# Layer 0's modulation tiles in a pool of their own, and the first pair's exponentials beside the v projection

## Chip, cores and metric

The kernel runs on one core of a Trainium2 chip. The metric is the device time of one execution in microseconds. Before the change it is 2110.99 us, the median of three runs from 2109.61 to 2111.64.

## What is computed

A block of four layers over 256 latent tokens and 256 context tokens of width 1024, with mixers A, B, C, A, each followed by a squared-ReLU MLP; every sub-layer has an RMSNorm, and shift, scale and gate come from a modulation product `silu(c) @ ada_w[l] + ada_b[l]`. The change is in mixer A, a bidirectional chunkwise mLSTM with 8 heads, chunks of 128 tokens and a scan in each direction. Cut to what matters:

```python
def mlstm_chunk_scan(q, k, v, log_i, log_f, state, with_output):
    def step(carry, inp):
        C, n, m = carry
        qc, kc, vc, li, lf = inp
        b = jnp.cumsum(lf, axis=-1)
        ...
        C_new = decay[..., None, None] * C + jnp.einsum('bhs,bhsk,bhsv->bhkv', ws, kc, vc)
        log_d = jnp.where(tri, b[..., :, None] - b[..., None, :] + li[..., None, :], -jnp.inf)
        d_mat = jnp.exp(log_d - m_comb[..., None])
        sc = jnp.einsum('bhtk,bhsk->bhts', qc, kc) * d_mat
        num = jnp.einsum('bhts,bhsv->bhtv', sc, vc) + a_inter[..., None] * jnp.einsum('bhtk,bhkv->bhtv', qc, C)
        ...

def mlstm_mixer(xc, xl, w_in, w_gate, b_gate, head_g, w_out, ctx_out):
    ...
    return (jax.nn.sigmoid(o) * h.astype(o.dtype)) @ w_out
```

## The kernel before

Every product with weights is done three times over a split in two parts: a weight tile of 128 x 1024 is loaded by SyncE (`w_dma`), cast to its high part by ScalarE (`w_hi`, line 241) and subtracted to its low part by VectorE (`w_lo`, line 246), and three matmuls (`mm3`, lines 390 to 392; for v lines 422 to 424) add high by high, high by low and low by high in one PSUM bank. `w_get(ahead)` makes the splits some tiles ahead; a split by `w_lo` also issues the load of the tile four further on. Weights are numbered in the order of use; in layer 0 the v projection uses 9 to 16 and the eight output-gate chunks use 17 to 24.

There is no scheduler: each engine carries out its instructions in the order in which the program writes them, and waits on semaphores for those of other engines. Tiles live in pools that are opened and closed like a stack on the left or the right side of the memory; a new tile waits for the last users of the tiles that lay in its place.

`mixer_a` of layer 0 projects keys, queries and gates, and then v in two halves of 512 columns (`nh`), each with four weight tiles (`kk`). The four PSUM banks of a half are copied into `vx` by ScalarE (line 789). The banks are taken in turn from six (`bank`); the scan then names its banks itself: the output-gate chunks go into bank 4, the key transposes into bank 5, the scores into 6 and 7.

Beside the projections, `pump` works off the modulation of layer 0. `ada_pe` does 16 of its tiles (`first`, in the pool `first`) on TensorE. `ada_pump` does 12 more (`ada`) as two sums each on VectorE (line 353, 24 in all), reading the tile and the broadcast conditions `cbc` and writing into `junk`; these two lie in the pool `first` as well. The tiles come through a ring of two, each loaded by SyncE when the one before it in its place is done.

`gates` computes the gate rows on 40 partitions in the pool `rows`, and writes two of them to DRAM (`dnm`, `dar`). `scan_load` (lines 882 and 883) issues, on GpSimd, four row loads `rb` and two `ab` for a pair of heads, broadcast to 128 partitions; `scan_qa` (lines 891 and 892) multiplies `ab` by the queries. In layer 0 both were called at the start of `scan`, with tiles in the scan's own pool `as0`, which opens when `rows` and `first` have closed. In layer 3 they have a pool `al3` from the start, and the loads of two pairs are issued in the gate steps.

`scan` goes over four pairs of heads. For a pair and a direction, `weights` adds a triangular mask to each of two `rb` tiles (VectorE, line 957) and takes exponentials of their chunks (ScalarE, line 959). `scores` makes the score matmuls (line 967) and transposes the keys (line 972); `keys_weigh` weighs the transposed keys (VectorE, line 982), `weigh` multiplies the exponentials by the scores (line 990), `states` makes the state products (TensorE, line 1000), `outputs` the outputs (lines 1025 and 1034). `fillers` lays the halves of the output-gate chunks between them, and copies each from bank 4 (line 912). Before the change `scan` began like this:

```python
        if not last:
            self.scan_load(lp, 0, dnm, dar, n, last)
            self.scan_qa(lp, 0, qT, n)
        for d in range(2):
            weights(0, d)
        scores(0)
        next(fill)
        keys_weigh(0)
        for d in range(2):
            weigh(0, d)
```

Of the kernel before, what the change touches and what calls it, by code (L numbers as in the profile page):

```python
# [8 lines left out]
F32 = mybir.dt.float32  # L9
F32R = mybir.dt.float32r  # L10
BF16 = mybir.dt.bfloat16
I32 = mybir.dt.int32
AF = mybir.ActivationFunctionType
ALU = mybir.AluOpType
# [4 lines left out]
D = 1024  # L19
# [11 lines left out]
N_FIRST = 4  # L31
PE_ADA = 32
# [40 lines left out]
def mixer_a_units():  # L73
    return [("k", 0), ("k", 1), ("k", 2), ("k", 3), ("q", 0), ("gate", 0), ("q", 1), ("q", 2), ("q", 3)]
# [133 lines left out]
class Body:  # L208
# [70 lines left out]
    def ada_fetch(self, j):  # L279

        if j < PE_ADA:
            t = self.ada_raw[j] = self.first.tile([128, 1024], F32, tag="first", name=f"first{j}", bufs=N_FIRST)
            (self.nc.sync if j < 16 + N_FIRST else self.nc.gpsimd).dma_start(out=t, in_=self.ada_in[j])

    def ada_rows(self, j, t):
# [76 lines left out]

    def conditions(self, pool):

        self.cbc = pool.tile([128, 2, 1024], F32, name="cbc")
        self.nc.gpsimd.dma_start(out=self.cbc, in_=self.line.unsqueeze(0).to_broadcast([128, 2, 1024]))
        self.junk = pool.tile([128, 1024], BF16, name="junk")

    def new_mod(self, l):
        self.mods[l] = self.modp.tile([128, 48, 2], F32, tag="mod", name=f"mod{l}")  # L370
# [336 lines left out]
    def mixer_a(self, l, i, last):  # L707
        nc, tc = self.nc, self.tc
        full = LT if last else ALL
        n = full.stop  # L710
        units = mixer_a_units()
        with ExitStack() as st:
            ap = self.block_pool(st, f"a{l}", "left")
            qT = ap.tile([128, 4, 512], F32, name="qT")
            kT = ap.tile([128, 4, 512], F32, name="kT")

            def ev_qk(u, o, sl):
                kind, m = units[u]
                if kind == "k":
                    nc.scalar.copy(kT[:, m, sl], o)  # L720
                else:
                    nc.scalar.activation(qT[:, m, sl], o, AF.Copy, scale=0.125)

            n_head = yield 3, ev_qk
            n_head = n_head or 3
            dr = st.enter_context(tc.tile_pool(name=f"ad{l}", bufs=1, space=DRAM))
            av = self.block_pool(st, f"av{l}", "left")
            vx = av.tile([128, 4, 8, 129], F32, name="vx")
            tok = av.tile([128, 3, 4, 64], F32, name="tok")
            if l == 0:  # L730
                saved = self.hin
            else:
                saved = dr.tile([128, 8, n], F32, name="saved")
                nc.gpsimd.dma_start(out=saved, in_=self.h[:, :, :n])
            nc.gpsimd.memset(vx[:, :, :, 128:129], 1.0)
            lp = self.block_pool(st, f"al{l}", "left") if last else None
            rows_ctx = tc.tile_pool(name=f"ar{l}", bufs=1, side="left", reuse_waits="tile")
            rows = rows_ctx.__enter__()
            steps = None

            count = [0]

            def pump():
                if l == 0:
                    count[0] += 1
                    if count[0] % 2 == 0:
                        self.ada_pe()
                    if count[0] > 3:
                        self.ada_pump(2 if count[0] % 4 == 0 else 1, 0, ADA_A)

            for u in range(n_head, len(units)):
                if units[u][0] == "gate":
                    w = self.w_get()
                    o = self.bank()
                    self.unit(o, w, self.x_chunk, ALL, range(4))
                    pump()
                    self.unit(o, w, self.x_chunk, ALL, range(4, NK))
                    steps = self.gates(rows, dr, i, o, last)
                    next(steps)
                    pump()  # L760
                else:
                    self.chunk(u, self.x_chunk, full if units[u][0] == "q" else ALL, ev_qk, pump)
                    pump()
                    if steps is not None:
                        rowt = next(steps)
                        if rowt and last:
                            for pr in range(2):
                                self.scan_load(lp, pr, rowt[3], rowt[4], n, last)
                            self.scan_qa(lp, 0, qT, n)

            for nh in range(2):
                outs = [self.bank() for _ in range(4)]
                for kk in range(4):
                    w = self.w_get()
                    self.v_step(w, 2 * kk, outs, 512)
                    pump()
                    self.v_step(w, 2 * kk + 1, outs, 512)
                    if nh == 0 and kk == 3:
                        u_, er, wr, dnm, dar = rowt
                        tp = self.bank()[:, 0:480].rearrange("p (a c r) -> p a c r", a=3, c=4)  # L780
                        for qi, t_ in enumerate((u_, er, wr)):
                            for tcn in range(4):
                                nc.tensor.transpose(tp[:, qi, tcn, :], t_[:, tcn * 128 : tcn * 128 + 128], self.ident[0:40, 0:40])
                        nc.scalar.copy(tok[:, :, :, 0:40], tp)
                    pump()
                for tcn in range(4):
                    dst = vx[:, tcn, nh * 4 : nh * 4 + 4, 0:128]
                    src = outs[tcn].rearrange("p (h v) -> p h v", h=4)
                    nc.scalar.copy(dst, src)
            rows_ctx.__exit__(None, None, None)  # L790
            if l == 0:
                while self.epos <= PE_ADA:
                    self.ada_pe()
                self.ada_pump(96, 0, ADA_A)
                self.first_ctx.__exit__(None, None, None)
            sp = self.block_pool(st, f"as{l}", "left")
            self.scan(l, i, last, sp, lp or sp, dnm, dar, qT, kT, vx, tok, saved, n)
        res = self.residual(l, 16, n)
        for m in range(3, 8 if last else 5):
            self.chunk(m, self.x_chunk, full, res, ahead=2 if last else 4)  # L800
        yield None if last else (self.x_chunk, res, (5, 6, 7))
# [83 lines left out]
    def scan_qa(self, lp, pr, qT, n):  # L885
        nc = self.nc
        for d in range(2):
# [3 lines left out]
            nc.gpsimd.tensor_copy(dc, a.rearrange("p (c t) -> p c t", c=4)[:, :, e])  # L891
            nc.gpsimd.tensor_tensor(out=a[:, :n], in0=a[:, :n], in1=qT[:, pr, :n], op=ALU.mult)

    def scan(self, l, i, last, sp, lp, dnm, dar, qT, kT, vx, tok, saved, n):


        nc = self.nc
        full = slice(0, n)
        outc = [0, 1] if last else [0, 1, 2, 3]
        nch = len(outc)  # L900
        masks = (self.mask_f, self.mask_b)
        bk = self.banks
        sg = self.h
        cur = self.cur
# [44 lines left out]


        def weights(pr, d):

            for hh in range(2):
                e = cur["D", pr, d, hh]
                col = 32 * d + 2 * pr + hh
                e3 = e.rearrange("p (c t) -> p c t", c=nch)
                nc.vector.tensor_tensor(out=e3, in0=e3, in1=masks[d].unsqueeze(1).to_broadcast(e3.shape), op=ALU.add)
                for c in outc:
                    nc.scalar.activation(e3[:, c, :], e3[:, c, :], AF.Exp, bias=tok[:, 0, c, col : col + 1])

        def scores(pr):

# [127 lines left out]
            )  # L1090

        fill = fillers()
        if not last:
            self.scan_load(lp, 0, dnm, dar, n, last)
            self.scan_qa(lp, 0, qT, n)
        for d in range(2):
            weights(0, d)
        scores(0)
        next(fill)
        keys_weigh(0)  # L1100
# [4 lines left out]
        for pr in range(4):  # L1105
# [15 lines left out]
            if more:  # L1121
                weights(pr + 1, 0)
# [7 lines left out]
            if more:  # L1130
                weights(pr + 1, 1)
                low()
# [370 lines left out]
    def start(self, n_head, evac_head):  # L1503

        nc = self.nc
        self.first_ctx = self.tc.tile_pool(name="first", bufs=1, side="right", reuse_waits="tile")
        self.first = self.first_ctx.__enter__()
        with self.tc.tile_pool(name="start", bufs=1, side="right", reuse_waits="tile") as sp:

            nc.vector.memset(self.cs, 0.0)  # L1510
# [7 lines left out]
            first = []  # L1518
# [94 lines left out]
            nc.gpsimd.tensor_copy(sp.tile([128, 2], F32, name="after"), self.mods[0][:, 4, :])  # L1613
            for s in range(2):
                nc.gpsimd.dma_start(out=line[s].rearrange("(k p) -> p k", p=128), in_=sg[:, 8 * s : 8 * s + 8])
            self.conditions(self.first)
            for j in range(N_ADA):
                self.ada_dma(PE_ADA + j)
            self.modulate2(0, 0, 4)
# [132 lines left out]
```

## Time and profile before

| what | value |
|---|---|
| median of three runs | 2110.99 us |
| lowest and highest run | 2109.61 and 2111.64 us |
| the profiled execution | 2114.74 us |
| its span, first to last instruction | 2113.0 us |
| busy: PE, DVE, ACT, POOL | 97%, 69%, 45%, 4% of the span |
| mean granted clock of TensorE | 0.990 |
| share of PE in the chain that ended last | 92% |

PE is TensorE, PEld its weight loads, DVE VectorE, ACT ScalarE, POOL GpSimd, SP SyncE; a q behind a name is the engine's sequencer. Times are in microseconds from the start of the span. A row of the timeline gives start, duration, engine, line, operation, output and inputs with their shapes, the count of merged instructions, and in brackets how long the engine stood idle before it and who ended that. Neighbouring instructions of an engine overlap a little, so the duration of one is somewhat longer than its distance to the next. The granted clock is 1.00 at 2.4 GHz and 0.50 at 1.2 GHz.

### The profile page before, as it was taken

How to read it: one execution, taken by the hardware profiler on the slowest of the kernel's cores; microseconds unless marked ns; L12 is line 12 of the kernel's file. 1: busy time of each engine (PE TensorE's matmuls, PEld its weight loads, DVE VectorE, ACT ScalarE, POOL GpSimd, SP SyncE). 2: the span in 40 equal slices, each digit the busy share in tenths (PEclk: the TensorE clock that was granted, in tenths of full speed). 3: DMA queues.
4: the chain of work that ended last, by engine and by line, in shares of the span. 5: the costliest groups of instructions: out<-in, count | busy, mean ns of one | idle time of the engine just before them, and what ended most of it. 6: DMA issues, size and time to landing. Idle time of an engine off the chain costs nothing.

```text
span 2113.0 us, 30325 instructions
## 1 busy us (share of the span) xinstructions
PE 2053.4 (97%) x11730; PEld 1751.2 (83%) x11730; DVE 1453.5 (69%) x2652; ACT 948.9 (45%) x1814; POOL 87.0 (4%) x138
## 2 busy tenths in 40 slices
PE   6989999999999999999999999999999999989998
PEld 4767798888889878988888988898888899889997
DVE  5667777787777775677777764467777776576554
ACT  3436653324236685624333343262433435556554
POOL 0123100000000000000000000000000000310000
PEclk9999999999999999999999999999999999999999
DMA  9783245565553104266565433236556533635552
GB/s 300 272 264 103 64 135 179 177 193 185 184 170 119 50 2 138 92 189 189 179 194 175 130 112 98 94 108 189 187 180 197 179 122 104 175 103 180 184 185 91
DMA packets 97025, 326.11 MB, mean 154 GB/s; under 512 B 17760, under 2 KB 18928, under 8 KB 96240
## 3 DMA queue, kind: packets, MB, share of 16 engines
q1 hardware_dynamic: 81184, 293.81, 43.5%
q0 software_dynamic: 15152, 29.83, 4.6%
q8 instruction: 92, 1.51, 0.3%
q10 hardware_dynamic: 544, 0.52, 0.1%
q14 instruction: 53, 0.43, 0.1%
HBM read 319.73 MB, written 4.33 MB: 153 GB/s over the span
## 4 chain that ended last, share of the span: by engine, by line
PE 92%; DVE 3%; DMA 2%; ACT 2%; issue 1%; POOL 0%; SPq 0%; DVEq 0%; ACTq 0%
PE bank L390 25%; PE bank L392 25%; PE bank L391 25%; PE bank L591 2%; PE bank L592 2%; PE bank L594 2%; PE bank L422 1%; PE bank L1348 1%; PE bank L423 1%; PE bank L424 1%; PE bank L1360 1%; DMA ab<-dar 1%; PE bank L1288 1%; PE bank L1025 1%; DVE wlo L246 1%; PE bank L1000 1%
## 5 line engine op out<-in xcount | busy, mean ns | idle before, releaser
L390 PE MATMUL bank<-xh,whi 128*128 128x512 f32 (+1 forms) x1600 | 579.4, 362 | 1.7 <-ACT h L912 1.0
L241 ACT CAST whi<-raw 128x1024 fp32r<-128x1024 f32 x374 | 387.1, 1044 | 421.1 <-PE bank L391 382.8
L391 PE MATMUL bank<-xl,whi 128*128 128x512 f32 (+1 forms) x1600 | 574.4, 359 | 0.2
L392 PE MATMUL bank<-xh,wlo 128*128 128x512 f32 (+1 forms) x1600 | 573.9, 359 | 0.0
L246 DVE TENSOR_TENSOR wlo<-raw,whi 128x1024 fp32r<-128x1024 f32 x374 | 455.6, 1225 | 152.5 <-ACT whi L241 151.9
L353 DVE SCALAR_TENSOR_TENSOR junk<-ada,cbc 128x1024 bf16<-128x1024 f32 x320 | 390.7, 1221 | 18.1 <-DMA ada<-in_ada 13.8
L390 PE MATMUL bank<-hh,whi 128*128 128x512 f32 (+1 forms) x1096 | 384.5, 351 | 0.0
L392 PE MATMUL bank<-hh,wlo 128*128 128x512 f32 (+1 forms) x1096 | 383.9, 350 | 0.0
L391 PE MATMUL bank<-hl,whi 128*128 128x512 f32 (+1 forms) x1096 | 383.9, 350 | 0.0
L390 PEld LDWEIGHTS bank<-xh,whi 128*128 128x128 f32 x1600 | 304.9, 191 | 49.9 <-ACT h L912 1.6
L392 PEld LDWEIGHTS bank<-xh,wlo 128*128 128x128 f32 x1600 | 304.9, 191 | 44.3
L391 PEld LDWEIGHTS bank<-xl,whi 128*128 128x128 f32 x1600 | 305.0, 191 | 44.0 <-DVE xl L945 1.0
L391 PEld LDWEIGHTS bank<-hl,whi 128*128 128x128 f32 x1096 | 207.4, 189 | 27.4
L392 PEld LDWEIGHTS bank<-hh,wlo 128*128 128x128 f32 x1096 | 207.4, 189 | 27.2
L390 PEld LDWEIGHTS bank<-hh,whi 128*128 128x128 f32 x1096 | 207.4, 189 | 27.1
L565 DVE SCALAR_TENSOR_TENSOR h<-bank,mod,h 128x256 f32<-128x256 f32 x280 | 125.6, 479 | 133.1 <-PE bank L392 133.1
L676 DVE TENSOR_TENSOR hl<-q,hh 128x512 fp32r<-128x512 f32 (+1 forms) x137 | 81.5, 595 | 170.5 <-ACT q L675 170.2
L673 ACT ACTIVATE r<-bank 128x512 f32<-128x512 f32 (+1 forms) x137 | 70.8, 517 | 269.2 <-PE bank L392 266.2
L459 ACT ACTIVATE sq<-h 128x256 f32<-128x256 f32 (+1 forms) x74 | 36.0, 487 | 139.4 <-DVE h L565 114.2
L591 PE MATMUL bank<-xh,whi 128*128 128x256 f32 x312 | 81.4, 289 | 3.5 <-ACT xh L527 3.5
L592 PE MATMUL bank<-xh,wlo 128*128 128x256 f32 x312 | 80.2, 285 | 0.0
L674 ACT ACTIVATE hh<-r 128x512 fp32r<-128x512 f32 (+1 forms) x137 | 75.9, 554 | 4.6
(274 smaller groups left out, 2129.3 us busy)
## 6 DMA issues: line engine op xcount, KB each, us to landing
raw<-in_wts SPq DMA_DIRECT2D x374, 512.0 KB, 4.2
ada<-in_ada SPq DMA_DIRECT2D x160, 512.0 KB, 3.5
start<-in_ada SPq DMA_DIRECT2D x16, 512.0 KB, 9.1
first<-in_ada POOLq DMA_DIRECT2D x12, 512.0 KB, 6.0
cbc<-line POOLq DMA_DIRECT2D x4, 1024.0 KB, 7.8
rb<-dnm POOLq DMA_DIRECT2D x16, 256.0 KB, 7.1
ab<-dar POOLq DMA_DIRECT2D x16, 256.0 KB, 12.2
h<-in_hin SPq DMA_DIRECT2D x4, 512.0 KB, 6.8
```

Of the source, the lines that this page charges most:

```text
L241: self.nc.scalar.copy(hi, self.raw[j])
L246: self.nc.vector.tensor_tensor(out=lo, in0=self.raw.pop(j), in1=hi.bitcast(F32), op=ALU.subtract)
L353: nc.vector.scalar_tensor_tensor(out=junk, in0=w, scalar=1.0, in1=self.cbc[:, s, :], op0=ALU.mult, op1=ALU.mult, accum_out=self.mods[l][:, ...
L390: mm(out, lhsT=whi, rhs=xhi, start=first, stop=False)
L391: mm(out, lhsT=whi, rhs=xlo, start=False, stop=False)
L392: mm(out, lhsT=wlo, rhs=xhi, start=False, stop=last)
L565: self.nc.vector.scalar_tensor_tensor(out=self.h[:, m, a:b], in0=o[:, a - sl.start : b - sl.start], scalar=mod[:, gate + m, s : s + 1], in ...
L591: mm(o[:, :T], lhsT=w[0][:, c], rhs=hi[:, sl], start=(k == 0), stop=False)
L592: mm(o[:, :T], lhsT=w[1][:, c], rhs=hi[:, sl], start=False, stop=False)
L673: nc.scalar.activation(r[:, :n], o, AF.Relu)
L674: nc.scalar.activation(hh[:, sl], r[:, :n], AF.Square)
L676: nc.vector.tensor_tensor(out=hl[:, sl], in0=q[:, :n], in1=hh[:, sl].bitcast(F32), op=ALU.subtract)
```

## The change

`first` now holds only `cbc` and `junk`; the ring of modulation tiles for TensorE gets a pool `tiles` that is opened above it and closed, with `rows`, after the first weight tile of v's second half. There the pool `al0` is opened on the left side, and `scan_load` and `scan_qa` of the first pair are called. `weights` is taken apart into `scan_mask` and `scan_exp`, and for the first pair these are called within v's second half: direction 0 behind the third weight tile, direction 1 behind the fourth, in layer 0 and in layer 3. `scan` no longer begins with them. In layer 0 the loop that drained `ada_pe` is gone.

```diff
@@ ada_fetch
-            t = self.ada_raw[j] = self.first.tile([128, 1024], F32, tag="first", name=f"first{j}", bufs=N_FIRST)
+            t = self.ada_raw[j] = self.tiles.tile([128, 1024], F32, tag="first", name=f"first{j}", bufs=N_FIRST)
@@ conditions
-        self.cbc = pool.tile([128, 2, 1024], F32, name="cbc")
+        if pool:
+            self.cbc = pool.tile([128, 2, 1024], F32, name="cbc")
+            self.junk = pool.tile([128, 1024], BF16, name="junk")
         self.nc.gpsimd.dma_start(out=self.cbc, in_=self.line.unsqueeze(0).to_broadcast([128, 2, 1024]))
-        self.junk = pool.tile([128, 1024], BF16, name="junk")
@@ mixer_a, in the loop over v
                     pump()
+                    if nh == 1 and kk == 0:
+                        rows_ctx.__exit__(None, None, None)
+                        if l == 0:
+                            self.tiles_ctx.__exit__(None, None, None)
+                            lp = self.block_pool(st, f"al{l}", "left")
+                            self.scan_load(lp, 0, dnm, dar, n, last)
+                            self.scan_qa(lp, 0, qT, n)
+                    if nh == 1 and kk >= 2:
+                        self.scan_mask(0, kk - 2)
+                        self.scan_exp(0, kk - 2, tok, [0, 1] if last else [0, 1, 2, 3])
                 for tcn in range(4):
                     dst = vx[:, tcn, nh * 4 : nh * 4 + 4, 0:128]
                     src = outs[tcn].rearrange("p (h v) -> p h v", h=4)
                     nc.scalar.copy(dst, src)
-            rows_ctx.__exit__(None, None, None)
             if l == 0:
-                while self.epos <= PE_ADA:
-                    self.ada_pe()
                 self.ada_pump(96, 0, ADA_A)
                 self.first_ctx.__exit__(None, None, None)
             sp = self.block_pool(st, f"as{l}", "left")
-            self.scan(l, i, last, sp, lp or sp, dnm, dar, qT, kT, vx, tok, saved, n)
+            self.scan(l, i, last, sp, lp, dnm, dar, qT, kT, vx, tok, saved, n)
@@ new, taken out of weights
+    def scan_mask(self, pr, d):
+
+        for hh in range(2):
+            e3 = self.cur["D", pr, d, hh].rearrange("p (c t) -> p c t", t=128)
+            mask = (self.mask_f, self.mask_b)[d].unsqueeze(1).to_broadcast(e3.shape)
+            self.nc.vector.tensor_tensor(out=e3, in0=e3, in1=mask, op=ALU.add)
+
+    def scan_exp(self, pr, d, tok, outc):
+
+        for hh in range(2):
+            e3 = self.cur["D", pr, d, hh].rearrange("p (c t) -> p c t", t=128)
+            col = 32 * d + 2 * pr + hh
+            for c in outc:
+                self.nc.scalar.activation(e3[:, c, :], e3[:, c, :], AF.Exp, bias=tok[:, 0, c, col : col + 1])
@@ scan
-        if not last:
-            self.scan_load(lp, 0, dnm, dar, n, last)
-            self.scan_qa(lp, 0, qT, n)
-        for d in range(2):
-            weights(0, d)
         scores(0)
@@ start
+        self.cbc = self.first.tile([128, 2, 1024], F32, name="cbc")
+        self.junk = self.first.tile([128, 1024], BF16, name="junk")
+        self.tiles_ctx = self.tc.tile_pool(name="tiles", bufs=1, side="right", reuse_waits="tile")
+        self.tiles = self.tiles_ctx.__enter__()
...
-            self.conditions(self.first)
+            self.conditions(None)
```

The orders of TensorE, GpSimd and SyncE are the same before and after; those of ScalarE and VectorE change at the end of v, in layers 0 and 3. A number behind an underscore tells buffers apart and is not the same in both programs; the number right behind `whi`, `wlo` or `raw` is that of the weight.

ScalarE in layer 0, from the cast for the second output-gate chunk on, before (`rb` are the exponentials of the first pair, `vx` the copies of v's second half):

```order
L241 CAST whi18_1004<-raw18_824 128x1024
L241 CAST whi19_1041<-raw19_869 128x1024
L241 CAST whi20_1076<-raw20_907 128x1024
L789 COPY vx_528<-bank_84 128x4x128 x4
L959 ACTIVATE rb_1116<-rb_1116,tok_529 128x128 x4
L959 ACTIVATE rb_1118<-rb_1118,tok_529 128x128 x4
L959 ACTIVATE rb_1122<-rb_1122,tok_529 128x128 x4
L959 ACTIVATE rb_1124<-rb_1124,tok_529 128x128 x4
L241 CAST whi21_1185<-raw21_966 128x1024
```

The same place with the change:

```order
L241 CAST whi18_1030<-raw18_827 128x1024
L241 CAST whi19_1067<-raw19_872 128x1024
L915 ACTIVATE rb_1013<-rb_1013,tok_532 128x128 x4
L915 ACTIVATE rb_1015<-rb_1015,tok_532 128x128 x4
L241 CAST whi20_1112<-raw20_910 128x1024
L915 ACTIVATE rb_1019<-rb_1019,tok_532 128x128 x4
L915 ACTIVATE rb_1021<-rb_1021,tok_532 128x128 x4
L800 COPY vx_531<-bank_84 128x4x128 x4
L241 CAST whi21_1192<-raw21_969 128x1024
```

Eight exponentials moved ahead of the cast of weight 20, and all sixteen ahead of the copies of v.

VectorE at the same place, from the last two modulation sums (`junk`) on, before (`kw` are the key weights):

```order
L353 SCALAR_TENSOR_TENSOR junk_372,mod0_146<-ada43_1023,cbc_370 128x1024 x2
L378 TENSOR_TENSOR mod0_146<-mod0_146,vecs_85 128x8
L246 TENSOR_TENSOR wlo20_1077<-raw20_907,whi20_1076 128x1024
L957 TENSOR_TENSOR rb_1116<-rb_1116,cons_86 128x512
L957 TENSOR_TENSOR rb_1118<-rb_1118,cons_86 128x512
L957 TENSOR_TENSOR rb_1122<-rb_1122,cons_86 128x512
L957 TENSOR_TENSOR rb_1124<-rb_1124,cons_86 128x512
L982 TENSOR_TENSOR kw_1177<-bank_84,tok_529 128x512
```

The same place with the change:

```order
L353 SCALAR_TENSOR_TENSOR junk_115,mod0_151<-ada43_1049,cbc_114 128x1024 x2
L379 TENSOR_TENSOR mod0_151<-mod0_151,vecs_85 128x8
L907 TENSOR_TENSOR rb_1013<-rb_1013,cons_86 128x512
L907 TENSOR_TENSOR rb_1015<-rb_1015,cons_86 128x512
L246 TENSOR_TENSOR wlo20_1113<-raw20_910,whi20_1112 128x1024
L907 TENSOR_TENSOR rb_1019<-rb_1019,cons_86 128x512
L907 TENSOR_TENSOR rb_1021<-rb_1021,cons_86 128x512
L998 TENSOR_TENSOR kw_1184<-bank_84,tok_532 128x512
```

The split of weight 20 moved behind the first two of the four masks; nothing else moved.

## Rows read from the trace of the kernel before

**Rows 1.** The page, part 1: busy us of each engine, share, instructions.
```profile
PE 2053.4 (97%) x11730; PEld 1751.2 (83%) x11730; DVE 1453.5 (69%) x2652; ACT 948.9 (45%) x1814; POOL 87.0 (4%) x138
```
**Rows 2.** Timeline of PE, layer 0, start of the scan.
```profile
143.37 0.66 PE L972 MATMUL bank<-cons,kT 128*128 128x128 f32 x4
...
149.10 0.39 PE L392 MATMUL bank<-xh,wlo 128*128 128x512 f32 x1
154.84 0.70 PE L1000 MATMUL bank<-vx,kw 128*64 128x129 f32 x4 [5.35 <-DVE rb L990]
155.77 2.42 PE L1000 MATMUL bank<-vx,kw 128*64 128x129 f32 x20 [0.22 <-DVE rb L990]
...
170.51 0.50 PE L390 MATMUL bank<-xh,whi 128*128 128x512 f32 x1 [1.02 <-ACT h L912]
...
179.26 1.54 PE L1000 MATMUL bank<-vx,kw 128*64 128x129 f32 x24
```
**Rows 3.** Waits of DVE, 125 to 150: total us, times, longest.
```profile
DVE junk L353 <- DMA ada<-in_ada: 9.8, 3, 3.7
```
**Rows 4.** Timeline of DVE, layer 0, start of the scan.
```profile
148.31 1.22 DVE L246 TENSOR_TENSOR wlo<-raw,whi 128x1024 fp32r<-128x1024 f32 x1
149.44 2.49 DVE L957 TENSOR_TENSOR rb<-rb,cons 128x512 f32<-128x512 f32 x4
151.85 1.15 DVE L982 TENSOR_TENSOR kw<-bank,tok 128x512 f32<-128x512 f32 x2
152.91 1.88 DVE L990 TENSOR_TENSOR rb<-rb,bank 128x512 f32<-128x512 f32 x3
155.03 0.69 DVE L990 TENSOR_TENSOR rb<-rb,bank 128x512 f32<-128x512 f32 x1 [0.24 <-ACT rb L959]
```
**Rows 5.** Timeline of ACT, layer 0, v and the start of the scan.
```profile
119.86 2.06 ACT L789 COPY vx<-bank 128x512 f32<-128x512 f32 x4
...
131.50 1.05 ACT L241 CAST whi<-raw 128x1024 fp32r<-128x1024 f32 x1 [4.85 <-PE bank L424]
...
140.34 2.63 ACT L789 COPY vx<-bank 128x512 f32<-128x512 f32 x4 [2.34 <-PE bank L424]
150.21 4.78 ACT L959 ACTIVATE rb<-rb,tok 128x128 f32<-128x128 f32 x16 [7.24 <-DVE rb L957]
154.90 1.03 ACT L241 CAST whi<-raw 128x1024 fp32r<-128x1024 f32 x1
```
**Rows 6.** Timeline of POOL, layer 0: the first pair's row loads.
```profile
118.11 0.54 POOL L882 DMA_DIRECT2D rb<-dnm  x1 [11.81 <-PE bank L783]
...
122.09 0.87 POOL L883 DMA_DIRECT2D ab<-dar  x1
```
**Rows 7.** Timelines of ACT and PE, layer 3, start of the scan.
```profile
1822.88 2.45 ACT L959 ACTIVATE rb<-rb,tok 128x128 f32<-128x128 f32 x8
...
1826.40 1.54 PE L1000 MATMUL bank<-vx,kw 128*64 128x129 f32 x24
```
**Rows 8.** Stretches: length, busy PE, PEld, DVE, ACT, POOL; PEclk, DMA share, GB/s.
```profile
154.90:160.90 6.00, 5.78 (x37) 5.04 (x38) 3.65 (x9) 2.46 (x4) 0.49 (x2) 0.50 0.55 161
195.05:198.50 3.45, 2.99 (x9) 2.57 (x10) 2.24 (x5) 0.89 (x2) 0.00 (x0) 0.51 0.30 119
222.40:229.20 6.80, 5.93 (x16) 4.87 (x17) 4.69 (x9) 2.24 (x4) 0.00 (x0) 0.50 0.20 72
```
**Rows 9.** Timeline of DVE, layer 0: masks of the second pair.
```profile
160.61 2.37 DVE L957 TENSOR_TENSOR rb<-rb,cons 128x512 f32<-128x512 f32 x2
...
166.82 1.28 DVE L957 TENSOR_TENSOR rb<-rb,cons 128x512 f32<-128x512 f32 x2
```
**Rows 10.** Weight loads: issue on SP; then landing times, 136 to 160.
```profile
129.36 0.33 SPq L235 DMA_DIRECT2D raw<-in_wts  x1
...
DMA to landing us min/median/max: 6.0/6.7/10.1
```

More of the change, by code (lines that the diff above doesn't have):

```diff
@@ L900, in scan @@
         nch = len(outc)
-        masks = (self.mask_f, self.mask_b)
         bk = self.banks
@@ L951, in weights @@
         def weights(pr, d):
[L953 to L959, printed above, removed]
+            self.scan_mask(pr, d)
+            self.scan_exp(pr, d, tok, outc)
         def scores(pr):
```

## The prediction

> **What bounds the kernel now.** I read the page's first part first: PE, the TensorE, is busy for 2053.4 of 2113.0 us [rows 1]. So a change can give or take only where PE stands still, and this one touches two such places at most: the start of the scan in layer 0 and in layer 3. I then read the timeline of PE there, asked which engine ends PE's wait, and went back along VectorE (DVE) and ScalarE (ACT), each in its own order.
>
> In layer 0 PE leaves v, does the first pair's scores, transposes the keys (143.37) and runs the first output-gate chunk behind them, whose last matmul starts at 149.10 [rows 2]. Then it stands for 5.35 us, until 154.84, and 0.22 us more. What it waits for is VectorE's last product of scores and weights (155.03, 0.69 us). VectorE comes late: in its order the modulation sums stand first, and from 125 to 150 us it waited 9.8 us in three waits for modulation tiles [rows 3]. So the first mask starts at 149.44 [rows 4], six microseconds after the key transposes, and masks, key weights and products follow it with only one gap, of 0.24 us. ScalarE stands idle for 7.24 us before the first exponential (150.21) [rows 5]; by then its four copies of v, which took 2.63 us from 140.34 on, are long done.
>
> **The pools move nothing.** GpSimd's list of instructions reads as before, and it already issues the first pair's row loads beside v: the first at 118.11, as soon as the gate rows' transposes let their memory go, the last of six at 122.09 [rows 6]. Opening the pool earlier in the program brings no load forward: cost and gain 0. This part of the change has no effect. SyncE's and PE's orders are unchanged too.
>
> **VectorE's order changes by one place.** The two masks of direction 0 now stand ahead of the split of weight 20 (the fourth output-gate chunk's), the two of direction 1 behind it. All 24 modulation sums still stand in front. So the first mask starts where that split started, at 148.31 [rows 4]: 1.1 us earlier and no more.
>
> **ScalarE's order is what costs.** The eight exponentials of direction 0 now stand ahead of the cast of weight 20, and the eight of direction 1 ahead of the four copies of v's second half. ScalarE is through with the cast of weight 19 at about 132.6 (131.50 and 1.05 us [rows 5]) and then waits for VectorE's mask, with the copies behind it. PE needs these copies: the second half of v fills banks 2 to 5 (six banks in turn, counted from the five heads on), the key transposes go into bank 5 and the output-gate chunk into bank 4. From the first mask at 148.31 the chain to the last copy is:
> - mask to first exponential 0.77 (150.21 less 149.44), eight exponentials 2.45 [rows 7]: 3.22
> - cast of weight 20, 1.03, and its split on VectorE, 1.22: 2.25. The split stands ahead of the other masks, so it is on the path
> - mask to exponential and eight exponentials again: 3.22
> - four copies, 2.06 [rows 5]
>
> Together 10.75, so the last copy ends at 159.06 and the transposes start there instead of at 143.37: 15.7 us later. The gate chunk, which ended at 149.5 (149.10 and 0.39), would end at 165.2 at full clock.
>
> **The clock.** Before, PE came back from its stall at half clock: 0.50 over the 6.0 us from 154.90, 5.78 of them busy [rows 8]. Two later stretches at 0.50 hold 2.99 and 5.93 us of busy PE. Half of such time is lost: 1.5 to 3.0 us. PE will have stood for 15.7 us and will come back at half clock, so now the gate chunk bears this; I take 2.3, the middle, and the chunk ends at 167.5. By then the key weights (two, 1.15) and four products (1.88 + 0.69), which can start at about 159.5, are done at 163.3. So the old stall of 5.57 is not paid again: it lies inside the new one.
>
> **From the state products on.** These 24 matmuls take 1.54 at full clock (179.26 [rows 2]) and end at 169.0; before, they ended at 158.2 (155.77 + 2.42), at half clock. That is 10.8 later. What follows, up to PE's next wait (until 170.51, for ScalarE), took 12.3 us and was bound by VectorE and ScalarE. Two masks in it took 2.37, where two others took 1.28 [rows 9]; up to 1.1 could go if what slowed them falls elsewhere, and I take 0.5 off. Net **+10.3 us**. From there on all is ordered as before, and PE, the bound, has no slack that could win it back. The bounds are +8.7 (1.5 for the clock, 1.1 off, 0.2 for overlaps of neighbours in the chain) and +11.5 (3.0, nothing off).
>
> The split of weight 20 comes about 4 us later (behind 3.22 and 1.03), and with it the issue of weight 24's load, the eighth gate chunk's, which is used in the last pair: nothing waits.
>
> **Layer 3** has the same swap with half the columns, no modulation sums, and a VectorE that is idle beside v. Its exponentials will lie beside v. But PE goes on into the state products at 1826.40 without a wait [rows 7], so the 2.45 us taken off ScalarE have nobody waiting for them: 0, and not more than 0.5 either way.
>
> **The queue in the trace and in the skill.** Weight 21's load was issued at 129.36, and loads there landed in at most 10.1 us [rows 10]; its cast nevertheless came at 154.90 [rows 5], right behind the exponentials. So a ready instruction stood behind a waiting one. The Trainium skill (PSUM — Partial Sum Buffer, Engine vs sequencer instructions) says that the queues of ScalarE and VectorE are strictly first in, first out; this row agrees, and by the rule the sum stays at +10.3. If copies could pass exponentials, the first rival's +2.8 would hold.
>
> **The rivals.**
> - *The copies are not in PE's way* (they pass, or the banks are others than I count). PE does its gate chunk as before and waits for the last product: the second masks start at 153.6 (148.31 + 3.22 + 2.25, less 0.2 of overlaps), take 1.2, then key weights and products 3.7: 158.5 against 155.7. +2.8: 2113.8. Against it: the transposes started at 143.37, right behind the copies that ended at 142.97 (140.34 + 2.63). Chance 0.04.
> - *Faster.* VectorE reaches the first mask so early that masks, exponentials and copies lie beside v. The place is the wait for modulation tiles. With the first mask by 132.2 the copies end by 142.97, and the 5.57 of stall and up to 3.0 of half clock go: 2102.4. From about 138.5 on, stall and delay are even, and only below that is anything won. But 138.5 is where VectorE would be if all 9.8 us of its waits vanished, and nothing in the change shortens them. Chance 0.03.
> - *A shorter wait.* The tiles land some microseconds earlier than in this one profile; each microsecond by which the first mask comes earlier takes one off. 2 to 6 us earlier gives 2115.3 to 2119.3. Against: the three runs lie within 2.0 us. Chance 0.07.
> - *Worse.* Half clock lasts beyond the gate chunk, or the next pairs fall behind as well, so that a later wait grows by 2 to 5 us: 2123 to 2127. Chance 0.05.
>
> **How the numbers follow.** The profiled execution took 2114.74 (span 2113.0), 3.75 above the median of 2110.99; I add the shift to the median. The forecast, +8.7 to +11.5 with a chance of 0.81, gives 2119.7 to 2122.5, and 2121.3 at +10.3. The range, 2116.5 to 2124.0, takes in most of the shorter wait and part of the worse case, and leaves out the other two. A measurement can tell about 0.2% (4.2 us) from no change: faster 0.03; same 0.04, and 0.01 of the shorter wait, 0.05; slower 0.92.
>
> **What would show it.** In the changed kernel's profile: row loads issued from about 118, modulation sums and their waits as before; first exponential near 149, after some 16 us of idle ScalarE that VectorE's mask ends; copies of v near 157 to 159; PE's long wait moved from the state products to the key transposes, about 15.5 us, ended by the copies, and none at the state products; half clock inside the first gate chunk; layer 3 unmoved. I am wrong if the copies run at 140 to 143, if the first mask comes much before 148, or if the transposes don't wait.

## The result, and the profile after

| set, each on one chip | before, median (runs) | changed, median (runs), lowest to highest | ratio, 95% interval |
|---|---|---|---|
| first | 2111.22 us (4) | 2123.40 us (4), 2121.93 to 2125.34 | 1.0057, 1.0044 to 1.0070 |
| later, beside the last experiments | 2111.68 us (12) | 2119.41 us (5), 2117.81 to 2121.94 | 1.0040, 1.0027 to 1.0053 |

The change makes the kernel slower, by 12.2 us in the first set and 7.7 in the second; both intervals lie above 1. The profiled execution of the changed kernel took 2124.73 us, 10.0 more than that of before (2114.74).

Its page begins like this:

```profile
span 2123.0 us, 30322 instructions
PE 2052.4 (97%) x11730; PEld 1749.7 (82%) x11730; DVE 1454.2 (68%) x2652; ACT 948.2 (45%) x1814; POOL 86.5 (4%) x138
```

PE is busy for 2052.4 us, against 2053.4 [rows 1]. The span is 10.0 longer, so PE stands still 11.0 more. Where it does so is told by its waits from 140 to 310 us (what PE waits for, total length, how often, the longest):

```profile
PE bank L988 <- ACT vx L800: 15.0, 1, 15.0
PE bank L988 <- DVE h L1104: 6.7, 2, 3.7
PE bank L1102 <- DVE h L1104: 3.2, 2, 1.6
PE bank L391 <- ACT h L934: 1.8, 1, 1.8
```

The first line is new: the key transposes (line 988 now, 972 before) wait 15.0 us for ScalarE's copies of v. The wait of the state products for VectorE's last product, 5.35 and 0.22 us in [rows 2], is gone. The timeline of PE shows the same place (the rest of the gate chunks left out):

```profile
158.41 1.11 PE L988 MATMUL bank<-cons,kT 128*128 128x128 f32 x4 [15.04 <-ACT vx L800]
159.18 0.78 PE L391 MATMUL bank<-xh,whi 128*128 128x512 f32 x1
...
166.99 1.54 PE L1016 MATMUL bank<-vx,kw 128*64 128x129 f32 x24
168.46 2.05 PE L1041 MATMUL bank<-vx,rb 128*128 128x129 f32 x16
170.44 0.72 PE L1050 MATMUL bank<-C,ab 64*128 64x129 f32 x8
...
180.35 0.50 PE L391 MATMUL bank<-xh,whi 128*128 128x512 f32 x1 [1.83 <-ACT h L934]
```

The transposes start at 158.41 instead of 143.37. The gate chunk behind them ends where the state products start, at 166.99, and these start without a wait and at full clock. The row at 180.35 answers to that at 170.51 in [rows 2]: from there on the program is the same, and PE is 9.84 us later. ScalarE's timeline says why the copies come so late:

```profile
131.45 1.05 ACT L241 CAST whi<-raw 128x1024 fp32r<-128x1024 f32 x1 [4.85 <-PE bank L425]
148.74 2.44 ACT L915 ACTIVATE rb<-rb,tok 128x128 f32<-128x128 f32 x8 [16.24 <-DVE rb L907]
151.09 1.03 ACT L241 CAST whi<-raw 128x1024 fp32r<-128x1024 f32 x1
154.01 2.44 ACT L915 ACTIVATE rb<-rb,tok 128x128 f32<-128x128 f32 x8 [1.89 <-DVE rb L907]
156.36 2.00 ACT L800 COPY vx<-bank 128x512 f32<-128x512 f32 x4
```

After the cast at 131.45 ScalarE stands for 16.24 us before the first exponential, and VectorE's mask ends that. Behind it stand the cast of weight 20, the other eight exponentials and the four copies, which ran at 140.34 before [rows 5]. VectorE, in the same stretch:

```profile
147.97 1.28 DVE L907 TENSOR_TENSOR rb<-rb,cons 128x512 f32<-128x512 f32 x2
152.15 1.22 DVE L246 TENSOR_TENSOR wlo<-raw,whi 128x1024 fp32r<-128x1024 f32 x1 [2.89 <-ACT whi L241]
153.29 1.29 DVE L907 TENSOR_TENSOR rb<-rb,cons 128x512 f32<-128x512 f32 x2
159.64 1.16 DVE L998 TENSOR_TENSOR kw<-bank,tok 128x512 f32<-128x512 f32 x2 [5.06 <-PE bank L988]
160.71 2.47 DVE L1006 TENSOR_TENSOR rb<-rb,bank 128x512 f32<-128x512 f32 x4
```

The first masks start at 147.97, 1.5 us earlier than in [rows 4]. Those of direction 1 come only at 153.29, since the split of weight 20 stands ahead of them and waits for ScalarE's cast. The modulation sums and their waits are as before: 9.6 us in three waits for tiles from 125 to 150 (9.8 in [rows 3]). The clock, from a table by stretches (columns as in [rows 8]):

```profile
143.80:149.00 5.20, 0.00 (x0) 0.00 (x0) 5.13 (x8) 0.26 (x1) 4.39 (x7) 0.78 0.69 218
149.00:159.00 10.00, 0.58 (x3) 0.59 (x4) 2.68 (x4) 8.11 (x22) 0.00 (x0) 0.50 0.84 239
160.00:165.00 5.00, 5.00 (x15) 3.92 (x15) 3.18 (x6) 0.00 (x0) 2.07 (x3) 0.62 0.04 12
165.00:170.00 5.00, 5.00 (x47) 4.20 (x46) 1.64 (x7) 1.53 (x2) 0.00 (x0) 1.00 0.00 0
180.89:184.30 3.41, 3.41 (x9) 2.63 (x8) 3.30 (x7) 1.61 (x3) 0.00 (x0) 0.50 0.27 103
```

The clock falls to 0.50 in the wait, and PE comes back at it: the transposes and the first matmuls of the gate chunk run at 0.50, until about 163.8. The state products and outputs, at 0.50 before [rows 8], run at 1.00. The last row is another stretch at half clock, right behind the 1.83 us wait at 180.35. GpSimd's row loads are unmoved: the first is issued at 118.06 and the last at 122.02 (118.11 and 122.09 in [rows 6]).

### The profile page after: what moved, and what is told of

Its sections match the earlier page's. It is cut to its first block, busy times and chain, and to the rows that moved or that the text cites. A ratio compares the mean times of both kernels' runs of the same rounds, so it can differ in the third digit from the quotient of the medians.

```text
span 2123.0 us, 30322 instructions
## 1 busy us (share of the span) xinstructions
PE 2052.4 (97%) x11730; PEld 1749.7 (82%) x11730; DVE 1454.2 (68%) x2652; ACT 948.2 (45%) x1814; POOL 86.5 (4%) x138
## 4 chain that ended last, share of the span: by engine, by line
PE 91%; DVE 4%; ACT 2%; DMA 2%; issue 1%; DVEq 0%; SPq 0%; ACTq 0%
PE bank L391 25%; PE bank L392 25%; PE bank L393 25%; PE bank L592 2%; PE bank L593 2%; PE bank L595 2%; DMA ada<-in_ada 1%; PE bank L423 1%; PE bank L1359 1%; PE bank L424 1%; PE bank L425 1%; PE bank L1371 1%; ACT rb L915 1%; PE bank L1299 1%; DVE wlo L246 1%
```

## The experiments

Two theories stood against each other. **A, the order on ScalarE:** exponentials that wait for VectorE stand in front of the copies of v, PE's key transposes need the copies, and VectorE is late because of the modulation sums. **The rivals:** the new pool and the early row loads cost something (B); layer 3, where the swap was made too, has its share (C); the masks beside v hold up VectorE's splits (D).

One number is compared throughout besides the time: in each trace, the distance from the first pair's score matmuls (142.28 in before) to the second pair's gate chunk (170.51). It holds all that the change touches in layer 0, and leaves out what differs between executions elsewhere.

### The pools and loads alone, and layer 3 alone

e1_pools takes the masks and exponentials back to the start of the scan; pools and loads stay as changed:

```diff
@@ mixer_a, in the loop over v
-                    if nh == 1 and kk >= 2:
-                        self.scan_mask(0, kk - 2)
-                        self.scan_exp(0, kk - 2, tok, [0, 1] if last else [0, 1, 2, 3])
@@ scan, ahead of scores(0)
+        for d in range(2):
+            weights(0, d)
```

> The changed kernel with its pools and its early row loads, but with the first pair's masks and exponentials back at the start of the scan, in layer 0 and in layer 3. Theory A (the copies of v stand behind exponentials that wait for VectorE, and TensorE waits for the copies): the pools move nothing, so this is the kernel before, 2111 within 2 us, with TensorE's wait of about 5.4 us at the state products and none at the key transposes. Rival B (the pools opened earlier, and the row loads under v, cost the time): it stays slow, 2120 to 2125.

Measured: 2112.86 us against 2112.53, ratio 1.0000 (0.9991 to 1.0008), and PE's wait is the old one again:

```profile
PE bank L1013 <- DVE rb L1003: 5.9, 2, 5.7
```

So the pools and loads cost nothing that can be measured. e4_layer3 does the swap in layer 3 alone:

```diff
-                    if nh == 1 and kk >= 2:
+                    if last and nh == 1 and kk >= 2:
@@ scan, ahead of scores(0)
+        if not last:
+            for d in range(2):
+                weights(0, d)
```

> Layer 0's first pair as in the kernel before, layer 3's masks and exponentials beside v as in the changed kernel. Theory A: layer 3 costs and gains nothing (TensorE did not wait there): 2111 within 2 us, and the waits of TensorE from 1800 on as in the kernel before. Rival C (a part of the 12 us is lost in layer 3): 2113 or more.

Measured: 2110.50, ratio 0.9990 (0.9981 to 0.9999). PE's waits from 1800 to 1960 us are those of before: 6.9 us at the key transposes for 6.8, then 3.5 and 0.9 in both, and smaller ones. In the changed kernel layer 3's first state products start at 1837.51 for 1826.40 in [rows 7], and the 11.1 us between the two are what PE was already late at the end of layer 0's pairs (253.27 for 242.18, a matmul behind the last pair). Layer 3 has no part in the loss.

### The order of ScalarE

e2_copies_first leaves the masks beside v and puts all exponentials behind the copies:

```diff
                         self.scan_mask(0, kk - 2)
-                        self.scan_exp(0, kk - 2, tok, [0, 1] if last else [0, 1, 2, 3])
@@ behind the four copies
+            for d in range(2):
+                self.scan_exp(0, d, tok, [0, 1] if last else [0, 1, 2, 3])
```

> The changed kernel with the masks beside v where the change put them, but all sixteen exponentials of the first pair behind the four copies of v. Theory A: the copies run at 140 to 143 again, the key transposes don't wait, and TensorE's wait is at the state products again, some 5 us: 2111 within 2 us. Rival D (it is the masks ahead of the split of weight 20, or that split being late, that costs): the masks still stand where the change put them, so half or more of the 12 us stays: 2116 to 2123. Rival B: 2120 to 2125.

Measured: 2110.45, ratio 0.9991 (0.9983 to 1.0000). A row of PE and two of ScalarE in this kernel:

```profile
143.26 0.66 PE L989 MATMUL bank<-cons,kT 128*128 128x128 f32 x4
140.23 2.63 ACT L799 COPY vx<-bank 128x512 f32<-128x512 f32 x4 [2.35 <-PE bank L425]
149.23 4.78 ACT L916 ACTIVATE rb<-rb,tok 128x128 f32<-128x128 f32 x16 [6.37 <-DVE rb L908]
```

The copies run at 140.23 as before, the transposes start at 143.26, and the whole loss is gone. Its masks start at 148.46, as late as in the changed kernel, and stand ahead of the same split. So the new place of the masks costs nothing, against rival D; that of the exponentials does. PE waits 5.6 us at the state products again.

e3_split_first keeps the exponentials where the change put them, and takes the split of weight 20 out of the path between the two directions:

```diff
+                    if nh == 1 and kk == 2:
+                        self.wsplit_to(self.wsplit + 1)
                     if nh == 1 and kk >= 2:
                         self.scan_mask(0, kk - 2)
```

> The changed kernel with cast and split of weight 20 ahead of the first pair's masks and exponentials; everything else as changed. Theory A: the chain from mask to last copy loses the cast and the split (1.03 and 1.22) and the second wait of ScalarE, but the first mask starts 1.1 later: the copies end some 2 us earlier than in the changed kernel, TensorE's wait at the key transposes is about 13 us instead of 15, and the time 2120 to 2122.5, against 2123.4. If the split were what costs (rival D), nearly all of the 12 us would go: 2111 to 2114.

Measured: 2123.26, ratio 1.0049 (1.0037 to 1.0060).

```profile
PE bank L990 <- ACT vx L802: 13.8, 1, 13.8
```

```profile
150.52 4.78 ACT L917 ACTIVATE rb<-rb,tok 128x128 f32<-128x128 f32 x16 [12.52 <-DVE rb L909]
155.20 2.00 ACT L802 COPY vx<-bank 128x512 f32<-128x512 f32 x4
```

PE waits 13.8 us for the copies instead of 15.0, and the 16 exponentials run in one piece. The wait came out near what was expected, the time 0.8 us above its band, and far above rival D's. Taking the detour over cast and split out shortens the wait by 1.2 us net, since the first mask now starts 1.8 later (149.75); the rest is VectorE's lateness and the exponentials themselves.

e8_one_direction puts only direction 1's exponentials behind the copies:

```diff
-                        self.scan_exp(0, kk - 2, tok, [0, 1] if last else [0, 1, 2, 3])
+                        if kk == 2:
+                            self.scan_exp(0, 0, tok, [0, 1] if last else [0, 1, 2, 3])
@@ behind the four copies
+            self.scan_exp(0, 1, tok, [0, 1] if last else [0, 1, 2, 3])
```

> The changed kernel with the exponentials of direction 0 ahead of the copies of v, as changed, and those of direction 1 behind them. Theory A: the chain ahead of the copies loses eight exponentials (2.4), the second masks and the second wait; the copies end at about 154.5 instead of 158.4, TensorE's wait at the key transposes is about 11 us instead of 15, and the time about 4 us under the changed kernel's: 2117 to 2120.5 where the kernel before takes 2111 to 2112.5. If the copies' place did not matter: as the changed kernel, 2122 to 2125.

Measured: 2115.69, ratio 1.0020 (1.0011 to 1.0029). The order is what was expected:

```profile
147.66 2.44 ACT L917 ACTIVATE rb<-rb,tok 128x128 f32<-128x128 f32 x8 [16.33 <-DVE rb L909]
150.01 1.03 ACT L241 CAST whi<-raw 128x1024 fp32r<-128x1024 f32 x1
150.94 2.02 ACT L801 COPY vx<-bank 128x512 f32<-128x512 f32 x4
```

PE waits 10.8 us and then goes through to the state products (161.46). The time is 1.3 us below the expected band. The expectation took 4 us off the changed kernel's time as the first set had it (2123.4). The distance from scores to gate chunk, 141.04 to 174.82, bears the 4 us out: it is 5.6 us longer than before's, where the changed kernel's is 9.9 longer. What was too high was the median it was taken from, as the second set shows: 7.7 less about 4 is the 3.9 measured.

### VectorE's lateness

If VectorE is early, the same order must cost less. e6_after_10 is the changed kernel with ten instead of twelve modulation tiles on VectorE ahead of the scan; the sums of the other two are made later in layer 0, and the pump beside the MLP takes two sums in seven steps of eight instead of five of six, so that all are done in time:

```diff
-ADA_A = 12
+ADA_A = 10
@@ mlp, pump
-                    self.ada_pump(2 if step[0] % 6 else 1, l + 1)
+                    self.ada_pump(2 if step[0] % 8 else 1, l + 1)
```

> The changed kernel with 10 instead of 12 modulation tiles summed beside layer 0's v; the two others go to the MLP of layer 0, whose steps take one sum instead of two in every eighth place instead of every sixth, so that all are done in time. Theory A: VectorE loses four sums and its last wait for a tile, so the first mask starts at about 139 instead of 148, the copies end at about 149.5, TensorE waits about 6 us at the key transposes and nowhere else there: 2108 to 2114, beside 2111 to 2112.5 for the kernel before, so 9 to 12 us of the loss gone although ScalarE's order is as changed. Rival (ScalarE's order costs by itself, whenever the masks come): 2120 to 2125.

Measured: 2113.90, ratio 1.0011 (1.0003 to 1.0020). This is within the expected band. The first masks start at 139.14, the copies at 149.14, and PE waits 6.4 us:

```profile
PE bank L988 <- ACT vx L800: 6.4, 1, 6.4
```

The loss falls from 12.2 or 7.7 to 2.1 us with the first mask 8.8 us earlier, and is not gone, because the copies still stand behind all 16 exponentials. The same edit on the kernel before, e5_before_10:

> The kernel before with 10 instead of 12 modulation tiles beside layer 0's v, the two others in the MLP of layer 0 (one sum instead of two in every eighth step instead of every sixth). Theory A: the wait of 5.4 us at the state products in layer 0 is VectorE's lateness; masks start at about 140, products end before the gate chunk does at 149.5, the wait and the half clock behind it go: 2101.5 to 2106. Rival (the wait is bound by the row loads or the exponentials, or the sums cost as much in the MLP): 2109 to 2113.

Measured: 2105.73, ratio 0.9972 (0.9961 to 0.9984). The state products follow the gate chunk without a wait and at full clock:

```profile
148.94 1.54 PE L1000 MATMUL bank<-vx,kw 128*64 128x129 f32 x24
```

So before's own stall is VectorE's lateness too. Both edits also move four sums into the MLP; what they cost there was not measured by itself, but the distance falls by 7.2 and the median by 6.1. And e7_copies_10 has both edits, ten tiles and, as in e2_copies_first, all exponentials behind the copies:

> 10 modulation tiles beside layer 0's v, masks beside v as changed, all exponentials of the first pair behind the copies of v. Theory A: as the kernel before with 10 tiles, within 1.5 us, because TensorE waits for neither there: 2101 to 2106. Rival (masks beside v are worth something by themselves once VectorE is in time): 2 us or more under the kernel before with 10 tiles.

Measured: 2103.36, ratio 0.9961 (0.9948 to 0.9973). That is 2.4 us under e5_before_10, outside the 1.5 that theory A allowed and on the side of the rival, that masks beside v win something by themselves. In its trace PE doesn't wait between v and the state products, as in e5_before_10; a row of PE and two of ScalarE:

```profile
147.01 1.54 PE L1017 MATMUL bank<-vx,kw 128*64 128x129 f32 x24
```

```profile
137.93 2.63 ACT L799 COPY vx<-bank 128x512 f32<-128x512 f32 x4 [2.34 <-PE bank L425]
140.45 4.79 ACT L916 ACTIVATE rb<-rb,tok 128x128 f32<-128x128 f32 x16
```

### Once more, side by side

Two things were open: whether the first 12.2 us held a further loss, and, after e7_copies_10, whether masks beside v win something once VectorE is early. The changed kernel and the two with ten tiles ran again, unaltered, on one chip.

> The changed kernel once more, beside the kernel before on this chip. Theory A (one wait of 15 us at the key transposes in the place of one of 5.6 at the state products, and then as before) gives what the profiles show: PE is 9.8 us later at the second pair's gate chunk and 11.1 us later at the end of layer 0's scan, so a ratio of 1.0046 to 1.0053. The rival is that a further loss, which the one profile does not show, is part of the 12.2 us between the first medians: ratio 1.0058 or more. The wait at the key transposes is 13.5 to 15.5 us in either case.

Measured: ratio 1.0040 (1.0027 to 1.0053), below the expected band and far below the rival's. The wait is 15.5 us. A further loss is not seen again.

> The kernel before with ten instead of twelve modulation tiles on VectorE, once more. Expected as measured: ratio 0.9972, between 0.9962 and 0.9982.

Measured: 2105.19, ratio 0.9969 (0.9957 to 0.9981).

> Ten tiles, masks beside v, all exponentials behind the copies, once more and in the same call as the kernel before with ten tiles. If the masks beside v add something of their own once VectorE is early, this one is 1 to 3 us below the other (ratio 0.9955 to 0.9968); if not, the two agree within 1 us. With the copies out of the way and VectorE early, neither has a wait at the state products, so the plain theory gives no difference.

Measured: 2104.52, ratio 0.9964 (0.9950 to 0.9977), 0.7 us below e10_before_10_again. The two agree within 1 us, their intervals overlap in both sets, and their distances below differ by 0.2 us: that masks beside v win anything of their own is not shown. Both versions beat the kernel before, and the changed one.

All kernels by that distance:

| kernel | scores to gate chunk, us | less before's 28.23 | medians: this less before |
|---|---|---|---|
| changed, twice | 38.13, 37.96 | +9.9, +9.7 | +12.2, +7.7 |
| e1_pools | 28.04 | -0.2 | +0.3 |
| e4_layer3 | 27.67 | -0.6 | -2.0 |
| e2_copies_first | 27.67 | -0.6 | -2.1 |
| e3_split_first | 36.50 | +8.3 | +10.7 |
| e8_one_direction | 33.78 | +5.6 | +3.9 |
| e6_after_10 | 29.55 | +1.3 | +2.1 |
| before with ten tiles, twice | 21.02, 20.69 | -7.2, -7.5 | -6.1, -6.5 |
| e7, e11: copies first, ten tiles | 20.79, 20.50 | -7.4, -7.7 | -8.4, -7.2 |

Each median lies within 2.5 us of what its trace shows in this one stage. The mean of the changed kernel's two medians, +9.95, is close to the mean of its distances, +9.8.

## Why the prediction was right

**What bounds, and the wait that moves:** right. PE's long wait went from the state products to the key transposes, ended by the copies; a start 15.7 later was forecast, and 15.0 was measured (158.41 for 143.37). e2_copies_first shows the cause: with the copies in front, the same late masks cost nothing.

**The pools move nothing:** right, by the issue times (118.06 to 122.02) and by e1_pools.

**VectorE's order:** the first mask at 147.97 for 148.31; the sums in front of it and their waits are unchanged.

**The chain of 10.75 us:** right within 0.4: from 147.97 to the end of the copies, 158.36 (156.36 and 2.00), it took 10.4. Its parts stand in the rows in the order forecast: mask to exponential 0.77, eight exponentials 2.44, cast and split at 151.09 and 152.15, mask to exponential 0.72, 2.44 again, copies 2.00.

**First in, first out:** PE had finished v when the scores began at 142.22, and the copies of its banks ran at 156.36, behind exponentials that waited for a mask. The copies were ready and did not pass them. The Trainium skill says of these queues that they are strictly first in, first out (PSUM — Partial Sum Buffer, Engine vs sequencer instructions); this trace agrees, and so does e2_copies_first, where the copies stand in front and run at 140.23.

**The clock:** 2.3 us was taken from bounds of 1.5 to 3.0. From the transposes to the chunk's last matmul it took 8.26 us (158.41 to 166.67), and 5.73 at full clock in [rows 2] (143.37 to 149.10): 2.5 lost. That PE would come back at half clock was reasoned from the old stall and came out; that the middle of the bounds came within 0.2 was luck. The chunk ended at 167.1 (166.67 and 0.39) for a forecast of 167.5.

**From the state products on:** they ended at 168.53 (166.99 and 1.54) for 169.0, 10.3 later than before where 10.8 was forecast: the chain was 0.36 shorter and began 0.34 earlier, and the clock took 0.2 more. The following chain up to 180.35 took 11.82, as forecast (12.3 less 0.5). Outputs at full clock freed PE 1.3 us sooner (from 168.46 to 171.09 is 2.63; in before the same took 3.97, from 158.11 to 162.08, mostly at half clock), but PE's wait for ScalarE at its end grew from 1.02 to 1.83. So the stretch is bound by VectorE and ScalarE, as the prediction had it. The 0.5 comes from the masks, as it supposed: they took 1.28 for 2.37, and from their start to the end of the exponentials behind them it took 3.18 (170.96 to 174.14) for 3.68 (160.61 to 164.29).

**+10.3 us:** 9.84 in the profile at that point, and 12.2 and 7.7 in the two sets, whose intervals both hold 10.3. The two medians lie on either side of the stated bounds, 0.7 above +11.5 and 1.0 below +8.7; the distances of the two traces, +9.9 and +9.7, speak for the forecast's size. So the mechanism is borne out, and the bounds were too narrow for one median: the three runs within 2.0 us that the prediction went by gave too small a scatter, as twelve later runs of before go from 2108.05 to 2115.84. The first median is 2.1 above the forecast time; which of the sets came nearer was luck. The intervals of the two sets overlap, and whether anything but scatter parts them is open. "PE has no slack that could win it back" held on the whole: at the end of layer 0's pairs the profile is 11.1 later (253.27 against 242.18) and at the end of the span 10.0. The difference is half clock: the 3.41 us stretch at 180.89 was not foreseen, and in layer 3 before ran a 6.8 us stretch where the changed kernel ran 3.4. Such stretches vary between executions of the same program: in the second trace of the changed kernel the one behind 180 is missing, and layer 3 has 6.8 us. So they are no effect of the change that the runs can show.

**Layer 3:** 0 was forecast; e4_layer3 bears it out within what medians can tell, and the equal waits and the unchanged 11.1 us bear it out more closely.

**The rivals:** "the copies are not in PE's way" falls with the wait that names them. "Faster" fell because the first mask came at 147.97. Its break-even, the first mask at about 138.5, is not tested: in e6_after_10 the first mask came at 139.14, but beside scores that came 1.5 us later than in the changed kernel, and the chain took 12.0 us (to 151.16) instead of 10.4, since both pairs of masks took 2.4 us for 1.3. PE's wait of 6.4 us is a little more than the old 5.57, and the change cost 1.3 us by the distance and 2.1 by the medians. Making VectorE early helps the old order more in any case: with ten tiles it is 8.2 us faster than the changed one (2105.73 against 2113.90 in one set). "A shorter wait" is not what the second set's 7.7 comes from: the wait there was 15.5. Of "worse" the first trace has a part, the 3.41 us at half clock behind 180.35, and half of it, an estimated 1.7 us, was lost; the second trace has none of it.

## What to carry to other kernels

Work that is moved ahead on one engine to fill its idle time is put in front of everything that stands behind it there. Ask first what it waits for, then who waits for what is now behind it: here 4.9 us of exponentials, which waited on a late VectorE, held four copies that were ready, and PE, the bound, stood 15 us for them. Put instructions that another engine waits for in front of those whose inputs come late, and shorten the late chain itself: two modulation tiles less on VectorE ahead of the scan won 6 us (e5_before_10) where the reordering lost 10.

## What the runs showed of the hardware

Some operations on VectorE took much longer when they fell beside GpSimd's product `ab` by `qT`, and GpSimd's took longer too. In the changed kernel, GpSimd's rows and VectorE's:

```profile
142.10 2.26 POOL L900 TENSOR_TENSOR ab<-ab,qT 128x512 f32<-128x512 f32 x1
...
159.33 1.27 POOL L900 TENSOR_TENSOR ab<-ab,qT 128x512 f32<-128x512 f32 x1
```

```profile
142.01 1.23 DVE L353 SCALAR_TENSOR_TENSOR junk<-ada,cbc 128x1024 bf16<-128x1024 f32 x1
...
143.17 2.27 DVE L246 TENSOR_TENSOR wlo<-raw,whi 128x1024 fp32r<-128x1024 f32 x1
...
170.96 1.28 DVE L907 TENSOR_TENSOR rb<-rb,cons 128x512 f32<-128x512 f32 x2
```

And GpSimd's product beside the slow masks of [rows 9], in before:

```profile
160.83 1.60 POOL L892 TENSOR_TENSOR ab<-ab,qT 128x512 f32<-128x512 f32 x1
```

The split of weight 19 took 2.27, where others take 1.22, and the product beside it 2.26; at 159.33, beside operations of VectorE that read a bank, the product took 1.27. The two masks that took 2.37 beside it in before take 1.28 now that both products end ahead of them. Not every neighbour loses: the modulation sum at 142.01, which started just ahead of the product, kept its 1.23, and the product and the split took longer. So a swap of orders can win or lose a microsecond by what it puts side by side. The Trainium skill has the rule (SBUF — State Buffer, Who interferes with whom: a VectorE instruction with two inputs from SBUF contends with a GpSimd instruction that reads SBUF), and these rows agree.

Half clock came in places that the order of the program does not tell. In the changed kernel's two traces, the same program, PE waited 1.83 and 1.82 us at the same place. In the first, half clock followed for 3.41 us, in which a matmul took 0.63 us:

```profile
180.35 0.50 PE L391 MATMUL bank<-xh,whi 128*128 128x512 f32 x1 [1.83 <-ACT h L934]
...
181.36 0.63 PE L391 MATMUL bank<-xh,whi 128*128 128x512 f32 x1
```

In the second (e9_changed_again) full clock followed, and the same matmul took 0.40:

```profile
180.84 0.50 PE L391 MATMUL bank<-xh,whi 128*128 128x512 f32 x1 [1.82 <-ACT h L934]
...
181.66 0.40 PE L391 MATMUL bank<-xh,whi 128*128 128x512 f32 x1
```

Such stretches move one execution against another by some microseconds, so a change of 10 us is sized better by one stage's distance, or by several sets, than by one median.
